# A new instruction order for a three-branch decoder layer: small products counted dearer

## The chip, the cores and the metric

The kernel runs on one core of one Trainium2 chip. The metric is device microseconds from launch to end, the median of several runs. Before the change it is 2362.93 us (three runs, 2354.34 to 2368.78).

## What is computed

One decoder layer over 2048 tokens of width 1024, float32. The normalised input goes through one projection into three groups of eight heads of width 64 each; each group mixes along the tokens in its own way, is gated, and one output projection closes the layer.

```python
h = _rmsnorm(x, norm_w[l])
proj = (h @ w_in[l]).astype(F32)
p_gdn, p_rwkv, p_hgrn = _split(proj, (GDN_PROJ, RWKV_PROJ, HGRN_PROJ))
y_a = _gdn_branch(p_gdn, ...)     # conv, l2norm, chunked delta rule, triangular solve per chunk
y_b = _rwkv7_branch(p_rwkv, ...)  # token shift, data-dependent decay, delta-rule state
y_c = _hgrn2_branch(p_hgrn, ...)  # forget gate, outer-product state
y = jnp.concatenate([y_a, y_b, y_c], axis=-1)
x = x + y @ w_out[l]
return _rmsnorm(x, final_norm_w)
```

## The kernel before, in words

**Tiling.** Tokens are cut into four blocks `tb` of 512, heads into four pairs `p`. A unit is one block and one pair, so there are 16 units, named `tb_p` (0_0 to 3_3). Chunks are 32 tokens, 16 in a block.

**Projection products.** Large products have a stationary tile of 128x128 and 512 moving columns (256 at block edges). They write the tiles `mmrr`, `mmrk`, `mmrv`, `mmgk`, `mmgq`, `mmgv`, `mmhq`, `mmhf`, `mmhi`, `mmrg`, `mmgg`, `mmhg`, `mmwa`. Weights come over DMA in pieces (`wr`), ScalarE (ACT) takes the high part (`w[:, 0]`) and GpSimd (POOL) the low part (`split`, line 496); three products (high by high, high by low, low by high) make one float32 result. Of all PE work these are the ones that wait for little: weights and a free bank.

**Small products.** Inside a unit everything is made of products on 32x32 or 64x32 tiles with 32 to 128 columns, float32, two passes each: scores `r_sc`, `g_sc`, sums `g_ss`, `r_ss`, `h_d`, the two halves of the triangular solve `pX`, `pY` (line 999), `uW`, `GA`/`GB`, `MA`/`MB`, the state chain `pc` (16 steps, line 1073), outputs `r_po`, `g_p`, `h_po`, and transposes `g_ptk`, `g_ptv`, `r_px`, `g_px`, `h_px` and others.

**The solve of a unit.** After `g_sc` on PE, VectorE (DVE) makes `GA`, scales it, runs 15 dependent steps `slv`/`Tf`, widens to `Bu` and transposes to `TT` and `Bn` (lines 1022 to 1044). `Bn` is an operand of `pX` (line 1047). Between `g_sc` and `pX` PE has no work of this chain; what the order puts there is projection products and small products of neighbours.

**Order.** The body is written as threads, and the string `ORDER` fixes how they are interleaved; both stay. Each instruction that is recorded by a `Lane` (line 243; all of them have line 253 in the profile) gets its final place on its engine from the table `LANES`: for each of five engines (PE, DVE, ACT, POOL and the DMA queue of SP) a packed permutation of the program's order. `lay_down` (line 259) unpacks it and chains neighbours:

```python
first = np.cumsum(runs[0])
order = np.concatenate([np.arange(a, a + n) for a, n in zip(first, runs[1])])
for a, b in zip(order[:-1], order[1:]):
    tc.add_manual_dep(seen[b], seen[a].name, edge, reason="lay_down")
```

The table was written by a planner outside the kernel, which priced each operation; neither its prices nor its due times stand in the file. After `lay_down` comes a last stage outside the table (lines from 1512), the second half of the output projection and the final norm.

**Head.** `derive` (line 380) makes small tiles of at most 17 columns from the parameter tile `pr` (`omu`, `hw0`, `hkk`, `hka`, `hln`, `hhn`, `hgn`, `lbx` to `olb`, `nea`) on DVE with three ACT exponentials or logarithms. `block` (line 613) loads the rows of x (`xt`), normalises and transposes them (`pxt`). `decays` (line 697) makes `tba`, `gg`, the small products `pg`, and from them on ACT `gc`, `gam`, `egc`, `egl`.

Of the kernel before, what the change touches and what calls it, by code (L numbers as in the profile page):

```python
# [48 lines left out]
def consts():  # L49
# [20 lines left out]
    for i, l in enumerate(LEVELS):  # L70
# [66 lines left out]
        "K$}Wy`8w==27I~%xaRRfdJelhD=7a8uhh`fd;^uy!+aif7DUT=8_%RSu|5eaujI|>FX2txNcU1NuA>!H$0typU!ln~nO~%UFQYZUaXLMLcPaWM"
        "FXgP$$h-I>s^`(ps{BZ2bN(PVI;->3Fu$AkQD@#ymE4Qg!}fXnYZ^@Rc@aIp*MjXFe&@i~m(%aL9sV5)c21&;!A=D=0n74ylar-w`D&*lU*|YL"
        "wwmgxm6u|#$N77}wG>#gKvqf%_=iA|1`}<(jGp9ksfBv;Cv-ZmfM2^qOXH{qJn#tpmam{cb6+q!h5Ep=)8O;hcp}tQ1FyUb3zFcqj$Ve&R)NPP"
        "EdxIzXeAWe4}AQDZsFT#CWT<Nj(gIpbPZO{p>t^@e*w>C!0-~9#fSNRtUMEJ)zTR7m4WS5w3mC(XIupY9nj|>XjAF^URYj7W4Vcz(ms9|GxNaH"  # L140
        "BXk@5G9D+NMi<h9@Y4lQ=@=;QRH(2C{3S^#yB1jY@H-f_(DTs5FtC(_2fyS>Se$3Y?on2LTEZiY%2nj})CK6ihIjU&<?(eAeVX1EK1#65aB8E6"
        "@cb0Kax3K!KPt*D<?(b0&Ea3r&4`orJQ&eC0KWV?&e*}d@x@^HaX8vg>|O$os1v7(4eb(Xo#-$;-VTdiKul~!Q#$V>bJfykr7y?IJgZ!w^!gq&"
        "zYcqT1ormB+JndmYX2V80LF)4%}VgK8)~Zt?hkk?@<<0_crSNCY(CG2xE}ZhVW)p%<w5Yd4^j9Z?4W!!11By7@~eTd18kLmtv#@NFx1g3(Y}&L"
        "<J^pJ*PCvT$g6-7@4-_Od{j>huzrCktRK#sK%RJJE_SXFb*hY#MBklqh|B@-(AgM2&EJLQx9}=%!`Y8Q(@#L%D|r;`>yE6^#k8LIb{E*zY^AZE"
        ">faQ$lpiCzQ}FKr-iJ8WESxOoPL|m*^bTw8M?fDbnuL>;r(1yGFjT)lcI$(T(PHw(KjB4Xf7Y;-7RHlBShhiRNkr9!*yl2!`4TLx1GZ<-6!!%z"
        "o#5{@a-(9k1E_rTf%rco{Y<f@9adZc9BY6<d%P=9dsyFyw{Hm-EjW8O@>3QW`z$&U^W7xAy5aOLu%ij5PeTO0#EaqKHpKE=U~C4S{y2XYs=-WB"
        "HK>#5QbkpNC~-7)u16lK1ghtFx}Z|gG7GE@p;PG<sZnW~NSmRgabmNMn$O|u8nM0%W0w?1-C;}KGL}T1iZCt&-n)>G+kov#v>N1u6?8st1h#uI"
        "p3YCv-MoSCLnc{_96d^+(L+BLUU(mVRaxsasYa0|`=S~&Bg@_+*)!lH@J)YY&9yX@*V8n9hOR;et|sO?`9|n<9&|QOD#F$9?+R3d8T2+X#2frm"
        "S`4cz>13ea2rl!y9cmtc6LXUN&qF?2&kD^1@No#<3XoyD7=Be9ehJppVm>8Iza7)4!lATN4$gMs+s}aFUGTaJI{jMSE5$4lPc}(psVZBFjL{;a"
        "nb>P4kiEdyh)TDB2krM(6K8qsnigdqWR)AXaUst7l8Ulru^20-?f9}BwsfK6v0E3!?ivo^5tVN~g~AR4Y0@%RBNqHWbv8=f*pK`&-p1SrM4GZ*"  # L150
        "AzFmo&|+}BjI8c~k*)Bg%7IxEYui}GWxe32gmo(JKZUhjB|kiEV{8gM-2(4x@2MQFGN#s9SLq!`pVKTFQT|o=VF#G1FUk*{B@Q<6Wbn2VIrN*c"
        "Gz)qEOhiSicxDoPMXU48IOPx`OGndweEkJ>&eA|A<W%gt7M1u(xx0NIm83)%R!X`Xnu|x&M6@hC-xq6!2!jg6ZW~jLu}Inj&nD?QlPOdjU5}f<"
        "If$jXd^e)0f!6`!Sk$c7_#LTO(_#5#bRA~r!uxA+kK6>+Y=yr+g11$+RKCy|{-D+1yK;h3p33Yx`_%~kt?<$|uBMA%rBB`9gU!h1dHx(x+#A0`"
        ";fp+Ut=9XpS755H&UOl2UtrbokuupZg&L&wuIkWiyy*dS+Pc5->EJku5?xb!(M?uU(`YsBQp@>IxB=GFLURLL%vVYlk4H(3t*=o{sx(>rOD?FZ"
        "8ChW{l<+8WdI#%R8H=ZVs6ril060}&jWq|j0sSr>2#xkY^q10m-%^nV<Gda4a4J?w&lc^bz-d=ttPsy%j*}<B=QHs;0D8dx2Kj$E0sPmNU*>Ge"
        "4|49x9|7*oc&ewJ`JPTGAH^;6u-whhM;xsI$G@U>ei<1r509<IJ?boE)AKM|MWcByW%*O8<_~c{^c>DN;J$MfGQ`I;j`#8goLGmO@F09s3kCfJ"
        "_sv@81AMifLuV8ZbVl&&V1GF?l>+4xyj^bUH<5~)b8t7kg>R*w^N*0T$0KT{LTST*eJB)CPd}zRxDWp0Xhk~-jFr;E@P&$<+4LLmaVh<QAHp5{"
        "X8IZB^EEV|ZpXJ-x`&^oDPV01{8NViR^F3)(uatSwb=b*iS;CIb4T$s0bZRzFS1fsD|jC$k(5SF|3qq)`rD5DwjDO!&hu#@YQP=55r{X?c;16b"
        "{y6l1CuT~(VJmhYf|aL0<sQ!V$i=KHzg5t)`VXxN?_D$>e-0goX9ukhg&3#NLiyUouZxjuMxOlo)D!P(@$Ad)KB_{9mXmd^>=DW?z8SgZH!wTu"
        "{X&c{mXRYPeTGX3^IK_J!mLV|*|dH3@S8!kD9rh2p}bWiPsW~kR{fb`L(W*Dt=D6X)H5xBP1+OMgAI6!<8v{WlQVPBlCoW|4+V8-kh|tj&&Kg7"  # L160
        "77}84M#dTJm$07J7(&4p;nclvTTb37Tp9CD<MY90&RC)Gh47*$JjW6BF??wJ5!agkoG>y&Rz$em7=OO~K5e<x=QoJ&Ju^}>;V}#pw4{6AT3_%*"
        "0=c;GRzEe!ZjR`71~8VHJ#u1$#_9=DFNV{X-zt1nCSLKxB3Jm<->CJWcum`zHVSjC1sbuoC2cKrEqaAGG~X9{$BQXBV|<b^{3qx}qp3(W%I*f)"
        "IW1pk>s-U3YqY5&MLh*_l4HL2j7M7J+h)UxLf35LFcjQ{XbX*{DXX!9LNl@G)2+%xRmNb=*c=gB-RfNv$aE2Rsn`yx=~ycRhpvr3jbEeFD%EIv"
        "q8~0O0;5u`xzKndXU@|)JvZk6==A7&HBOmvL6MPdsaPv$(6zCq`YY_2k==fb<$~4CG8<U#Yh^`%8t&RyN*ivRqP!8t?2l&<Wl5>Ey}(o==IMlG"
        "AnxyoFE2LVN%|(6k#i;*T+4-PnD8aq(iY=DlQ}AFo-7kPqEYS`93f(AhO8`$sV!}Msv{<_Sxui3pn^qTWlWxRX_U>H2~^g|LnW{;fhy|87^^h9"
        "YK&TGKCJM~UzCegzRj5WrFB#sV}+a@h#y?5$rDXA@Wpdc_VkUPG<L^iR7cJaV|Agp8bmBbJf%%8DKPAsN>Iq2`b^)dJApfC#QW9O^RC4cn7H>%"
        "4RB4~3uN}%SQaQS<l5Ti+UgcqO%Aj=O&B}0H{GH*Q_m$uG3Fjq3F6tL&@^+t$<qH@oo=k2<!sCivzbEkGtpr4VvGbuH7!EsTNSDJ>}-7+`9Bro"
        "#EbO_^X-Gix|~E+l%2yOTXmLJUuE%hoK&W7#!?}#xrVv4Ae>?2(u>`z5@NsV6Lu!5JP8wRQADMU73v<S;>S1Z3R$N%mizS6G;>y2?1m8CaP%n+"
        "!hdv6{AR`SW0lLbH!Ig_@JTb1#oP9x>=$Y80+S_@rY<SfoFI3N3ZuEuFp`Y1<6HKM73RevRe7~ixQO3O<2AJkeWTG-5L@Y*h<9zg7e|R-6o*=0"
        "rS{HOP?sw?+$~a6vBJDqev8+oIp0!|zFl+rp5fXI;DBd+n{&+?*T%e7aN1_YoW+w7u3dvEp2IwITP=(N)3h(Oy=lu+Iu=WbSSE{Vns3finbwo1"  # L170
        "P)?7m(e`-eW)K>tJaf<0G1fDNqi{<JV)`xIr3%;!xAwr;8d={>Mk>}T>`kd~!}Y;oVDe$c?&ThH_i>9NOW7XS8(^i}$&rzr{{rUP5Hk"),
# [1447 lines left out]
```

## Time and profile before

| | |
|---|---|
| median of three runs | 2362.93 us |
| profiled execution | 2368.77 us |
| its span, first to last instruction | 2367.0 us |
| PE busy | 2204.5 us (93%) |
| DVE busy | 1482.6 us (63%) |
| ACT, POOL busy | 794.9 us, 677.1 us |
| mean granted TensorE clock | 0.977 |
| DMA | 145 GB/s |

PE is busy nearly all the time; its busy time counts modelled, overlapping spans of pipelined products, so it isn't PE at its peak. The rest of the span is PE idle: 2367.0 minus 2204.5 is 162.5 us.

### The profile page before, as it was taken

The page shows a single profiled execution, that of the slowest core. Times are in us where ns is not written, and L with a number is a line of the kernel's source. Part 1 is how long each engine was busy: PE and PEld are TensorE (multiplying, and loading weights), DVE is VectorE, ACT ScalarE, POOL GpSimd, SP SyncE. Part 2 cuts the span into 40 slices and gives each one's busy share as a digit, 9 for nine tenths or more (in the row PEclk, how much of TensorE's full clock was granted, in tenths as well). Part 3 has the DMA queues.
Part 4 walks back from the last instruction along what each step waited for, and adds up shares of the span by engine and source line. Part 5 has one row for each costly group of instructions (what it writes and reads, how often), then busy time and mean ns, then how long its engine had stood idle before and what let it go on. Part 6 is the DMA issues. An engine that isn't in the chain of part 4 may idle for free.

```text
span 2367.0 us, 86943 instructions
## 1 busy us (share of the span) xinstructions
PE 2204.5 (93%) x38264; PEld 1757.6 (74%) x38264; DVE 1482.6 (63%) x3430; ACT 794.9 (34%) x1586; POOL 677.1 (29%) x993
## 2 busy tenths in 40 slices
...
PEclk8999999989999999999999999999999999999999
...
GB/s 150 170 178 156 179 158 182 177 150 103 139 123 114 121 109 124 127 165 110 156 87 144 91 140 102 166 132 136 122 127 118 113 131 127 180 154 217 237 231 156
DMA packets 236363, 343.16 MB, mean 145 GB/s; under 512 B 22608, under 2 KB 99792, under 8 KB 235984
## 3 DMA queue, kind: packets, MB, share of 16 engines
...
q8 instruction: 300, 4.92, 0.9%
...
## 4 chain that ended last, share of the span: by engine, by line
PE 72%; DVE 14%; issue 5%; DMA 4%; ACT 3%; POOL 2%; SPq 0%; ACTq 0%; POOLq 0%; DVEq 0%
PE pa L253 6%; PE pc L253 5%; PE mmrk L253 4%; PE mmhq L253 4%; PE mmgv L253 4%; PE mmgq L253 4%; PE mmrv L253 4%; PE mmgk L253 4%; PE mmhf L253 3%; PE mmrr L253 3%; PE uW L253 3%; DMA wry<-ydram 2%; PE mmhi L253 2%; PE r_po L253 2%; DVE Tf L253 2%
## 5 line engine op out<-in xcount | busy, mean ns | idle before, releaser
L253 PEld LDWEIGHTS pc<-S,M 128*128 128x128 f32 x1024 | 145.1, 191 | 28.6 <-DVE S L253 6.7
L253 PE MATMUL pc<-S,M 128*128 128x64 f32 x1024 | 149.8, 269 | 3.0 <-DVE M L253 1.7
L253 DVE TENSOR_TENSOR S<-pc,S 128x128 f32<-128x128 f32 x256 | 73.4, 287 | 82.8 <-PE pc L253 79.8
L253 POOL TENSOR_TENSOR wy<-wry,wy 128x256 fp32r<-128x256 f32 x96 | 71.8, 759 | 92.1 <-ACT wy L253 90.6
L253 POOL TENSOR_TENSOR D<-gw,cst 128x512 f32<-128x512 f32 x64 | 71.4, 1116 | 83.7 <-DVE rawhg L253 34.1
L253 DVE SCALAR_TENSOR_TENSOR h_S<-h_S,tot 128x64 f32<-128x64 f32 x256 | 83.1, 325 | 14.9 <-ACT h_S L253 10.4
L253 PE MATMUL pa<-hhi,wy 128*128 128x512 f32 x224 | 74.3, 412 | 3.1 <-ACT wy L253 2.5
L253 ACT ACTIVATE wy<-wry 128x256 fp32r<-128x256 f32 x96 | 38.7, 416 | 113.7 <-DMA wry<-ydram 77.0
L253 DVE TENSOR_TENSOR Tf<-Tf,slv 128x15 f32<-128x15 f32 (+7 forms) x240 | 63.8, 266 | 6.4
L253 ACT ACTIVATE uW<-uW 128x1024 f32<-128x1024 f32 x32 | 32.8, 1025 | 95.3 <-PE uW L253 95.3
L253 DVE TENSOR_TENSOR slv<-Af,Tf 128x15 f32<-128x15 f32 (+7 forms) x240 | 60.5, 252 | 6.1
L253 PEld LDWEIGHTS h_l<-h_q,h_k 64*32 64x32 f32 x4096 | 41.4, 106 | 25.4 <-issue 12.2
L253 POOL TENSOR_TENSOR g_n<-g_n,mhalf 128x8 f32<-128x8 f32 x16 | 26.6, 1660 | 110.4 <-DVE g_n L253 110.4
L253 POOL TENSOR_TENSOR h_e<-h_k,h_q 128x512 f32<-128x512 f32 (+1 forms) x32 | 36.8, 1149 | 70.8 <-DVE h_q L253 46.6
L253 DVE COPY_PREDICATED h_P<-mlev,h_l 128x128 f32<-128x128 int32 x128 | 37.3, 296 | 27.0 <-PE h_l L253 26.8
L253 PE MATMUL h_l<-h_q,h_k 64*32 64x32 f32 x4096 | 48.8, 200 | 4.6 <-issue 2.4
L253 DVE TENSOR_TENSOR h_k<-h_k,tot 128x256 f32<-128x256 f32 x64 | 32.6, 510 | 32.3 <-PE h_l L253 32.0
L253 PE MATMUL pa<-whi,yl 128*128 128x512 f32 x128 | 50.0, 391 | 3.0 <-DVE yl L253 3.0
L253 DVE TENSOR_TENSOR M<-MA,D 64x512 f32<-64x512 f32 x64 | 43.9, 686 | 11.5 <-PE MB L253 8.9
L253 PEld LDWEIGHTS pa<-hhi,wy 128*128 128x128 f32 x224 | 41.6, 195 | 12.6 <-ACT wy L253 3.0
L253 PE MATMUL pa<-whi,yh 128*128 128x512 f32 x128 | 49.9, 390 | 0.1
L253 PE MATMUL pa<-wlo,yh 128*128 128x512 f32 x128 | 49.8, 389 | 0.0
...
## 6 DMA issues: line engine op xcount, KB each, us to landing
...
```

Of the source, the lines that this page charges most:

```text
L253: i = f(*a, **k)
```

## The change

Only the five packed strings in `LANES` are replaced. No instruction is added or removed: each table holds the same number of entries (22140 on PE, 3338 on DVE, 1515 on ACT, 973 on POOL, 1292 on SP). The packed text says nothing to a reader, so here is its shape, and then what comes out when it is unpacked and put beside the names of the recorded instructions.

```diff
 LANES = {
     "tensor": (
-        "c-nne36vGZ6@C4?fB)aJ;Gba|0j1#&GXuji0R;vSz77t{3@D>9ic3&*Jg(r8C?d%@F^VBZ;xQ(e=rJ+JEU38Q7MFyhqEQqO1R;Q86xkFN!Xg>|"
...
+        "c-nPV4RBP|6+XLf_w8<WldK7Z<xid@Bq0!pAb%~$5+H#D1T0cUElmr>3JA2;pQ43UEwoA*oZ25OgO=&Eb&9ARtU{R%+B#YRg|W&gMlG!fEiEde"
...
     "vector": (
...
     "scalar": (
...
     "gpsimd": (
...
     "sync": (
```

Instructions with another neighbour ahead of them than before: 1555 on PE, 1931 on DVE, 683 on ACT, 329 on POOL, 169 on SP. On PE a middle instruction is displaced by 6 places or fewer in half of the table, and by 296 at most.

**Projection products between the last `g_sc` and the first `pX` of a unit** (those of 256 columns count one half), units 0_0 to 3_3:

| | 0_0 | 0_1 | 0_2 | 0_3 | 1_0 | 1_1 | 1_2 | 1_3 | 2_0 | 2_1 | 2_2 | 2_3 | 3_0 | 3_1 | 3_2 | 3_3 | sum |
|---|---|---|---|---|---|---|---|---|---|---|---|---|---|---|---|---|---|
| old | 114 | 108 | 108 | 45 | 120 | 123 | 90 | 75 | 120 | 120 | 111 | 67.5 | 108 | 111 | 120 | 40.5 | 1581 |
| new | 111 | 111 | 96 | 39 | 117 | 114 | 81 | 73.5 | 108 | 126 | 87 | 60 | 108 | 120 | 108 | 51 | 1510.5 |

Counted from the product `pe` to `pX` the sums are 1482 and 1438.5, from `g_ptv` to `pX` 931.5 and 913.5, from `pX` to `pY` 123 and 118.5, from `pY` to the first `uW` 97.5 and 114. The small products inside the first of these stretches are nearly the same in both tables. DVE instructions from the last `GA` of a unit to its `Bn`, all units: 970 and 966.

**Stretches of small products** with no projection product and no transpose in them: 104 of 128 passes or more in the old table, 116 in the new; 13 and 20 of 192 passes or more.

**Head.** On SP the first part of `pr` moves behind the first tile of x, and the second part behind `wba`. On DVE the old order has `hw0`, `hkk`, then the first product row (`xt0_20`), then `xm0_3`, `omu`, `hka`, `lbx`, `hln`, `hgn`, `nea`, `hhn`, the difference `hlo`, the rows `xt0_30`, `xt0_31`, then `lbr`, a row, `lbs`, `lb`, `olb`; the new one has `hw0`, `xm0_3`, `omu`, the row `xt0_20`, `hkk`, `xt0_30`, `hka`, `xt0_31`, `hlo`, and only then `hln`, `hhn`, `nea`, `hgn`, `lbx`, `hka`, `lbr`, a row, `lbs`, `lb`, `olb`. On ACT the order `nea`, `hhi`, `lbe`, `hhi`, `olb`, weight split `w3wa` is the same; later the old order has `gc`, two `gam`, `egc` ahead of the split `w2wa`, and the new one has the splits `w2wa`, `w3wa`, `w0rr` ahead of `gc`. On PE the three `pg` stand ahead of the products with `w2wa` in the old order; in the new one two `pg`, three products with `w2wa`, the third `pg`, then the rest.

## Rows read from the trace of the kernel before

**Rows 1.** The page, part 1: the span, then busy time by engine.
```profile
span 2367.0 us, 86943 instructions
PE 2204.5 (93%) x38264; PEld 1757.6 (74%) x38264; DVE 1482.6 (63%) x3430; ACT 794.9 (34%) x1586; POOL 677.1 (29%) x993
```

**Rows 2.** The page, part 2: granted clock in 40 slices, in tenths.
```profile
PEclk8999999989999999999999999999999999999999
```

**Rows 3.** The chain that ended last, shares of the span by engine.
```profile
PE 72%; DVE 14%; issue 5%; DMA 4%; ACT 3%; POOL 2%; SPq 0%; ACTq 0%; POOLq 0%; DVEq 0%
```

**Rows 4.** Windows: busy time of each engine in head and tail, first the columns.
```profile
core 0: us, PE busy (x) PEld busy (x) DVE busy (x) ACT busy (x) POOL busy (x), PEclk, DMA share, GB/s
0.00:50.00 50.00, 27.67 (x246) 23.44 (x246) 22.60 (x58) 26.68 (x69) 16.06 (x42) 0.90 0.48 156
...
2050.00:2200.00 150.00, 141.57 (x1262) 110.23 (x1244) 52.56 (x99) 40.30 (x100) 74.58 (x94) 0.97 0.63 190
2200.00:2367.00 167.00, 151.32 (x648) 123.02 (x648) 80.97 (x93) 49.57 (x68) 18.63 (x28) 0.97 0.62 205
```

**Rows 5.** Waits of PE: total us, times, longest; by what was waited for.
```profile
PE pX L253 <- DVE Bn L253: 17.5, 13, 3.0
PE pxt L253 <- DVE xt L253: 16.5, 6, 7.4
PE g_p L253 <- issue: 10.4, 7, 2.0
PE GB L253 <- issue: 5.8, 3, 2.6
...
PE r_po L253 <- issue: 4.1, 3, 2.1
...
PE pY L253 <- issue: 4.0, 3, 1.7
```

**Rows 6.** Timeline of PE in the head: start, duration, what, idle before.
```profile
23.93 0.39 PE L253 MATMUL mmwa_0h<-hhi,w3wa_0h 128*128 128x256 f32 x1 [4.00 <-ACT w3wa_0h L253]
...
41.28 0.60 PE L253 MATMUL pg<-gg,cst 128*128 128x32 f32 x4 [4.10 <-issue]
...
44.48 0.58 PE L253 MATMUL mmwa_0h<-hhi,w2wa_0h 128*128 128x256 f32 x1 [2.30 <-ACT w2wa_0h L253]
```

**Rows 7.** Timeline of ACT in the head.
```profile
23.36 0.20 ACT L253 ACTIVATE olb<-olb 128x4 f32<-128x4 f32 x1
...
42.23 0.22 ACT L253 ACTIVATE gc<-pg 128x64 f32<-128x64 f32 x1 [1.49 <-PE pg L253]
...
44.03 0.41 ACT L253 ACTIVATE w2wa_0h<-wr2wa_0h 128x256 fp32r<-128x256 f32 x1
```

**Rows 8.** Timeline of SP in the head: the DMA issue of the parameters.
```profile
1.19 0.42 SPq L253 DMA_DIRECT2D pr<-par  x1
```

**Rows 9.** Timeline of PE around the first solve product of unit 1_2.
```profile
905.63 0.39 PE L253 MATMUL mmhg<-hhi,w1hg 128*128 128x512 f32 x1
...
906.99 0.39 PE L253 MATMUL mmhg<-hhi,w2hg 128*128 128x512 f32 x1
909.99 1.29 PE L253 MATMUL pX<-Bn,ATo 32*32 32x32 f32 x128 [2.61 <-DVE Bn L253]
```

**Rows 10.** The tile Bn: who writes it on DVE, 16 times.
```profile
L253 DVE STREAM_TRANSPOSE Bn<-Bu x16: 1040/1070/1135, 138.9 to 2016.3; 128x512 f32<-128x512 f32 x16
```

**Rows 11.** Timeline of PE: two groups of 16 small passes.
```profile
213.15 0.40 PE L253 MATMUL r_po<-uW,r_TL 32*32 32x64 f32 x16
...
213.60 0.40 PE L253 MATMUL r_po<-uW,r_TL 32*32 32x64 f32 x16
```

**Rows 12.** The page, part 3: the queue that brings instructions.
```profile
q8 instruction: 300, 4.92, 0.9%
```

**Rows 13.** Windows around two of the waits of Rows 5, columns as in Rows 4.
```profile
1026.00:1037.00 11.00, 7.28 (x273) 6.36 (x273) 8.12 (x15) 4.26 (x10) 2.35 (x5) 0.69 0.45 150
1530.00:1540.00 10.00, 7.50 (x285) 6.82 (x286) 7.22 (x13) 3.60 (x8) 2.48 (x5) 0.83 0.40 133
```

More of the change, by code (lines that the diff above doesn't have):

```diff
@@ L137 @@
[L137 to L171, printed above, removed]
@@ new lines @@
+        "S;cu03zY5O<E%~Zg1d<qJiA5r9lsJqWZcF-skN*-$9q2cF|@ajtX7M>o`B(Ob9CGb>QPF)w<lYTsKdWc_-Ca5p9=Ku1*e3gKmW9CRAec=#hB+x"
+        "^{gtmtC`cz;HfXVn|X>Z6}mH+-TI?n8F8da{U6{y1q1"),
+    "vector": (
+        "c-o~{S&ST46}|J`tKMfHk3D0I?TIa9659|5oR~Ev3P@r5Kp;L4;)6s22@psm`GhYNP*5Zg2!8lLLV(}{gjm9sMcKeM2}{CiX8}9TjK|LGz0Bp@"
+        "`(9O7*Hrg(+Zw&@>Z-Tgd+t5w-kKp|wp5@NN7TfXAsH<;_#B~SuF^VJ@I8!Ss758Kv&_BBV;GYp^B7OwOuxt6TKLuE0_~<vp1`UG)^746bR73A"
+        "{+gJ#mlk*j&0|=4Nw4<Nb9{jQ&99|r_z3-(XX!kbu+CyQ*f&Z`_$|9fu+D{Ziqv3#RiO=?YjJN4&l$6um}_zW0R0y;*5JnsPT5C`u<JRVqZfG("
+        "MgvzDxQ^?ySZB%6H0BrdT!w86Jf$lZ!gUEdF7XJ?ndfPet2I0^dbPx(@OU#=Ql(Y+zKY+&ilF~x=~m2k^mELAC;fy!KtEFa9%jMT(J*{!@Z<C;"
+        "{sZ4YC;5H!GdzDU{glO`IpDPm_8!FPf@ckDYQSeD;84bIIlZLzx44LJu|u9ntXA-pS>jy=K8B{?liVMJkMemLt7`b%g>z(|2(u^E|4TfMF+mZ2"
+        "P2zMHqBDWjmzXuyBYMIxa>j<($gCowx1gUZ9oR^2dF!gc&;nWU-~>I+@-6u|iam}1gX8ohpQJnZ6yFS-3>~Jw@L~EZON8G}5Av<_8@`jig?RYA"
+        "Dm1B{3POb>i@ZNg&7fj(*Wuh%V7P)IUM?#_RYaLt(A<Hjiai$lR^eZRWrbw8L)I-}H(A@jj;u%);Z+%{%NpekM54u`ipo5$$AN2+1j#zS$HLx{"
+        "A7agJJeB;K(o9=I=AKOu`yl<0KTJQs@6XYFd=EVQJa+gJ-J@1Iuyr0+a&`%}E@Cf<+99AhhR;iUo@bCZyXl;IG)=DnC5hH3ypM2I$2_kEavcTV"
+        "EcsZp*yC8o{@$Loz!syc7`7CEjSPz&M=(?3S?A9nE>?L9SCvyv_pIs+&&xHet_POLn1$ch(0@`x@Hm^~+}^<5J@h}|Ay=Xi64^R3caeobRiOMb"
+        "{FD=Fcvd9gainLDVqRL2B031|IY|G~@f!Mve#^<Pqo<UGHvvb<v}ui~tdQ*W>p8Kj9Q3FXz9Vv~r5u!%Rk^%=iA9lm-$EWs%tUFY>3QCdENH;T"
+        "bE<;z?mJ<<>@cPXy@Kz$=8Dtk_{@_m9ML?B6{m)oZN|w}MbBJU#8??Bdp7tNbPK<p{>0Z~FuwtNJ{_1QjNHn!b@jHOOsiqff-*_GFsi<uDN-wn"
+        "2^uz+YcXpq?VyW_l;@kQn9#^y!tTRZ)l4$72-ZoKEo<hC!OLUNgCq2Jcx^TA^IBId#j%O6EZt7O<ac4b2bg@HKT6-_SQjRd^B=<RN9kAm1+{rZ"
+        "6~#wuMs;-qzvCSx+r96RUVG0s1J0YkaZ@=trdBT_rq5%?ae6`huHlI&4fBR_xSaTHaMnxU>w>a>68<<6&8=XTJS_wjb95Z}DXWjFB0h^Vj?*8J"
+        "txsZ{3Rvs}?}g9adq<z7Z{TV#o_vJ9i6?iWHr&s5(Y<^x-NpAoS0(~0JonC^LZ0DU=y&`MRQa1R_8?A^+5>FB3$e&EzkpMGJiV%|BVs%7Dd<Yp"
+        "IjkF1q%J4*->ZUT<A!=B%oYAhF0E?31@%wB<`!4Ax=CJa1{EnN+cq>Va!M&&OO8oC?uJ6_Ms`U3nS+9O%OnmmtX9W$mRu6V8H~FC%xA#6S&jTA"
+        "e3A%9fh%I$!*nATl+ThC*I?KE7=n>>Fh}WW?Pg>MpF}y{LXQBirrK?3ME&x5D)y8SNuM)C?CFt|4BuqWmug4lc3NASs@YBKDoSt>zK((=h9uTI"
+        "HUE8|U?{%YsdyWm>ovFlZ{n)9uD1A`iYxXM=0-HCO0p7ID^`@lm7%z1%jt{kV|N{W1xj)Z*>{XitCF0~RBWl{Z=;8hQNQIo=-aSrO*6ZQ9GA1Q"
+        "S|V69*>kO5C6SKtVu+eeeU4+rNKnu?PfemIYub%?%@j=${kk4j9|g1WxO6*KRq1>DG5QXFoDR_4-0m?%OCF>X$_cCX&jw{Eke}g4g+#&Xs@7gd"
+        ";%tain|<wwEp@6a;>!xZT6?k=IPR(&+|pc<is0+5Lq0617D^Vlge!uzkHk}<Gd_a&Y@pITiw^uGzfmjRsg#zw93A~MeI3>Pe!d&A_+rwtiLNyG"
+        "%TST8(r2-5B3QQvUG=MAg;bLhu;dBEU7{!UL_tG@x%;*5onx;g)7r&&%smE+ut)5WUPe0D^Y|`nrbtZ1w~A(v^u%SYk7cOG*McTz^&_q|z7Mt9"
+        "-3z;#s@qaUBixI763NfG!0mWAjns_d>-(Y#e2%S_?pQLamC=zFve5VWHz||j_ad)L`}F<f3>YK*;UpMzf*#|yqW7KJq9W<Hp*CaMZ*=j~l5*XK"
+        "^R4E9M?sW)TorvWbR6<2tGsUXt0K~mG(xv%R84%}-_9K0pVmWF^j)&=6MY}zw3jYWwih|glAmv)NA(@(TKXFwLZ)_VNWc9^P5D*OY?J3psv;xc"
+        "`-@vN#3Sb`a}<!82yb|@s--<}zIv=8hmLh<M_x}NzSyKPd)|t2oT9^OO}hV>)1KgE?c*f|7ebvnr(J4#2v@2!t4xx;J)@)+-T*9*k+7*q(trLq"
+        "@tM`?%lbCyv7ANpntGbol7?oQ?_8Dwe`L@1qn8prSw(Gc>Ra#{zZ;%k2Yesk+vwN4tUjy(2dQK6dxythSb5geK5kO8@S;|=N_d-hxG(QQ@+t9^"
+        "o<ury>B?`UC$zTShI0f7(L=H5GGB|&L-bFr$Wz$EzX$sh8ystiyytoqmflL#*Y}t8@V^F$avZ6cV^Xi@=oz*l|82;Ca?nOUtFCHL2uzSn8p6CG"
+        "{WD>-e`WvDGc0V1?-%v6nwm9(6Fb*BeIhe!IlE@>h;5xSq8xjMdRp7<?qIu^j1ODyM}6&W`<i2VT2u{p#?=<n^>owKb29)YdAZ;Q#?*V|20D2w"
+        "+Wo|{7G{Wk#<}YH_N+HT@m-r*mEL`DRPxriT&DH2lj%UalEY=2pd-WNAYoFTrFR|Nx2R*C$-z77xvRZOHm6n1riSZ4*=79Q{%<s_vKfT(tTa9I"
+        "DjVMzeVgmOSHs>6YRAtF#LX+w)sb+DOPChh-j9m*6VWshHYX!ZN-Mq3HsoEmD%PD*wlD488DfyVZ-T8R6MNGGQPWlDyX954+)3xJO}J+>=h%)o"
+        "b=SqMe8}^t8lqp`VpsVJRIpbB%r?kHeKEHf>Q;VUx*qXz9lBvNy^QU%s>jNat{rY02J~N-21D3&^cbec?6w}6ZPnIYVcg@Y?KGCf6h^jdl^$G4"
+        "(hRXZ)HClC8+5KamwIP%d*!a&o~E<j+HG^7pN`IDv@?6k&=$SQ*3CldxyfK-dR9%B!`Ncd!KZtSN=mD?T3Q~c9`&bXSI44Kq6Ybz)a!kzv;XKk"
+        "(Iyye|2LMw$@Y=?z3bm#edeGlVtT$Wn2x#jDl}xckAB2#t01OlFWId#>#iOyr5)S7bF}Ao)4Xb`9u4*2aJnv=ocP(EeMi358XCHSF0tQ;mU38C"
+        "8ZbArZ!hhdG?D5Hx6kg*C{;2u3OUunBt1r2ztgrm+Cl#Z1Mq~h"),
```

129 lines of the change are left out of this document (62 added, 67 removed).

## The prediction

> **What bounds the kernel now.** I read the page first: PE is busy 2204.5 of 2367.0 us, DVE 1482.6, and no other engine is near [rows 1]. The chain that ended last says the same: 72% of it is PE's own work, 14% DVE's [rows 3]. The work itself isn't changed by a new order, so what the order can win or lose is PE's idle time, 2367.0 - 2204.5 = 162.5 us, and what the granted clock takes. The clock row shows full speed in most slices [rows 2]; its mean of 0.977 is worth 0.023 x 2367 = 54 us of the span if PE was busy all that time.
>
> Next I split the idle time. The windows give the head (first 50 us) 50 - 27.7 = 22.3 us, and the tail from 2050 us on (150 - 141.6) + (167 - 151.3) = 24.1 us [rows 4]. The waits of PE give two heaps in the middle: the solve products `pX` waited 17.5 us for DVE's `Bn` in 13 of the 16 units, and where the releaser is "issue" (PE waited for nothing that the profile shows) the four longest heaps `g_p`, `GB`, `r_po`, `pY` make 10.4 + 5.8 + 4.1 + 4.0 = 24.3 us [rows 5]. The rest, 162.5 - 22.3 - 24.1 - 17.5 - 24.3 = 74.3 us, is spread over many small waits. The reader should see that there is no large hole: 1% of the run is 23.6 us, more than either heap.
>
> **The solve windows.** This is the place where the old order's fit can be read. In 1_2 PE is through with its projection products at about 907.2 us and then stands 2.61 us until `Bn` is there [rows 9]. That `pX` waits in 13 of 16 units, but only 1.3 us on the mean and never over 3.0, shows that the old order has the two sides nearly level, PE a little early and DVE a little late. The new table takes projection products out of these windows: 70.5 fewer counted from `g_sc`, 43.5 fewer counted from `pe`, 18 fewer counted from `g_ptv`, while DVE's stretch from `GA` to `Bn` stays at 966 instructions against 970. That is what a dearer price for the small products would do: the same chain on DVE seems covered with fewer large ones. One projection product takes 0.227 us (six steps from 905.63 to 906.99 us [rows 9]), so PE arrives earlier by 70.5 x 0.227 = 16.0, 43.5 x 0.227 = 9.9 or 18 x 0.227 = 4.1 us in sum. `Bn` itself, a transpose of 1.07 us, comes no sooner [rows 10]. I take the middle anchor, +10 us of waiting, since DVE's chain runs from `pe` on by way of `E` and `GA`; the ends +4 and +16 stay for the range.
>
> [...]
>
> **Where the products go.** They stand elsewhere, since none is lost. From `pY` to `uW` there are 16.5 more (3.7 us), and no wait of `uW` is among the long ones [rows 5]. The others may stand ahead of one of the spread waits. Bounds: nothing, or all of the 9.9 us taken out of the solve windows. No row is nearer to either end; I take half, -5 us.
>
> **The issue waits.** The instruction queue brought 300 packets, 4.92 MB [rows 12], and PE's 38264 products and as many weight loads [rows 1] are 255 instructions for each packet. The waits called issue stand inside runs of small products [rows 5], which at 14 ns a pass use up the 128 passes of one packet in 1.8 us [rows 11]. Runs of at least 128 such passes go from 104 to 116, a factor of 1.12: 24.3 x 0.12 = +3 us. Runs of at least 192 go from 13 to 20: 24.3 x 0.54 = +13 us. I take +3, because the small groups are the same ones in nearly the same neighbourhood.
>
> [...]
>
> **The head.** The first part of `pr` takes 0.42 us on SP ahead of x [rows 8]; without it x starts at most 0.4 us sooner. The wait of 4.00 us for the split `w3wa` hangs behind `olb` on ACT, 23.36 us [rows 6, 7]. The new order puts `lbx`, the root of `olb`, later among the rows, and `xm0_3` and the rows earlier; these are operations of 0.1 to 0.7 us on either side, so I leave this wait as it is. The third wait goes: PE stood 2.30 us for the split `w2wa`, which ACT did at 44.03, behind `gc`, which had waited 1.49 us for PE [rows 6, 7]; now the split stands ahead of `gc`. The wait of 4.10 us ahead of `pg` stays, since `pg` needs `gg` and nothing ahead of `gg` is moved by much. At best -2.3 - 0.4 = -2.7 us, at worst 0, if the weights behind are late next; I take -2. If ACT's three splits delay `gc`, its dependants `gam` and `egl` are needed only in the next stage, so nothing on PE waits at once.
>
> **The tail.** Output products and the loads behind them keep their order but for the places near the last unit; I cost it at nothing, bounds -3 and +3, by the wait of `pa` that would move with it, which is under the 24.1 us of rows 4.
>
> **The sum.** -2 + 10 - 5 + 3 = +6 us. On the profiled execution's own 2368.8 us that is 2374.8; this execution lies 5.8 us above the median of the runs, so for the median 2362.9 + 6 = 2369 us.
>
> **The rivals.** A, faster: the table, made with truer prices, fits everywhere else, and half of the 74.3 us of spread waits goes, while solve, issue and head are as above: -37 + 10 + 3 - 2 = -26, 2337 us. For it speaks that these waits are many and short, so small shifts can close them; against it, that in the one place where I can measure the fit the shift goes the wrong way. It decides from 35 us of such waits closed (35 - 11 = 24), so nearly all of it is needed.
>
> B, slower: the solve waits grow by the whole 16 us of the `g_sc` anchor, nothing comes back elsewhere, and the longer waits pull the clock down. Around 1026 us the granted clock is 0.69 for 11 us, 3.4 us lost, and around 1530 us 0.83 for 10 us, 1.7 us lost, each time at a wait of PE [rows 13]. Eight units whose wait grows over 2 us would cost 8 x 1.7 = 14 us. 16 + 14 + 3 - 2 = +31, 2394 us. It passes 1% from the fourth such unit on (17 + 4 x 1.7 = 24). Against it: PE does more work in other windows and may meet DVE later everywhere.
>
> C: the issue waits take +13, not +3: +16, 2379 us. D: small products that alternate with other work take more than the 14 ns they take in a row [rows 11], so the new cover, with the same small products in it, is as long as the old one seemed: -2 + 0 - 5 + 3 = -4, 2359 us. [...] E: the changed parts of the head do nothing, since the weights set it: +8, 2371 us, which can't be told from the forecast.
>
> **How the numbers follow.** Forecast with E 0.42, C 0.08, D 0.10: together 0.60 for within 1%, which is about what a measurement here can tell from no change (2339 to 2387). A holds 0.20, B 0.20. The forecast's own range is 2355 to 2382. The range for 8 in 10 reaches from A to B, 2337 to 2394, and leaves out the further half of each.
>
> **What would show it.** Right: PE's busy time within 5 us of 2204; `pX` waits for `Bn` in all or nearly all units, 22 to 33 us in sum; no wait for `w2wa` over 1 us in the head; issue waits of 25 to 38 us. Wrong: a sum for `pX` under 17 us refutes the counting of the cover, and with it the sign; a granted clock under 0.965 means B; an idle time of PE under 140 us means A.

## The result and the profile after

The new order takes 2385.38 us (median of four runs, 2380.03 to 2388.15); the kernel before, beside it on the same chip, takes 2358.64. The ratio is 1.0105 [1.0074, 1.0136]. In a second comparison (run `again`, below) it was 1.009 [1.0064, 1.0116] with 2386.94 against 2365.74 us. So the change costs about 1%, 21 to 27 us. The time lies in the predicted range, in its upper part; the likeliest value, 2369, was missed by 16 us, and the time is also above the forecast's own range (2355 to 2382).

The page after, in the lines that answer to [rows 1 to 3]: span, busy time, granted clock in 40 slices, and the chain by engine.

```profile
span 2385.9 us, 86941 instructions
...
PE 2223.1 (93%) x38264; PEld 1772.9 (74%) x38264; DVE 1474.9 (62%) x3430; ACT 797.3 (33%) x1586; POOL 677.5 (28%) x993
...
PEclk9999999989999999999999998899999999899999
...
PE 68%; DVE 17%; issue 5%; DMA 4%; ACT 3%; POOL 3%; SPq 0%; POOLq 0%; ACTq 0%; DVEq 0%
```

PE's idle time is 2385.9 - 2223.1 = 162.8 us against 162.5 before: no change. PE's busy time rose by 18.6 us for the same 38264 passes, and that is the whole of the longer span (18.9 us). The same work took longer because the granted clock was lower:

```profile
core 0: 2385.9 us, clock 0.969
```

Against 0.977 before, that is (0.031 x 2385.9) - (0.023 x 2367.0) = 74 - 54 = 20 us. This pair of profiles gives the clock the most: over eight timed runs of the new order (1 - clock) x span is 66 us on the mean, over 25 runs of the old 57 us, so the clock's share over all runs is nearer to 10 of the 21 to 27 us. The other 11 to 17 us lie outside the clock, and this pair of profiles hides them: the profiled execution of the kernel before (2368.77 us) was the slowest of its four, 10 us above their median. The second profile of the new order (run `again`) is 15.9 us longer than the old order's: 8.7 us by the clock, 3.1 by waits over 0.1 us, and some 4 us that stay without a place.

The waits of PE, as in [rows 5]: total us, times, longest.

```profile
PE g_p L244 <- issue: 18.5, 10, 3.1
...
PE pX L244 <- DVE Bn L244: 12.4, 9, 3.0
PE GB L244 <- issue: 7.6, 6, 2.6
PE r_po L244 <- issue: 5.8, 5, 1.9
...
PE pX L244 <- DVE xm L244: 3.1, 1, 3.1
```

`pX` waits less than before, not more (12.4 + 3.1 = 15.5 against 17.5 us). The waits called issue grew: `g_p`, `GB` and `r_po` had 20.3 us, now 31.9; the fourth heap of [rows 5], `pY`, fell from 4.0 to 1.6. Summed from the trace between 115 and 2125 us ("the middle" from here on: PE's idle times over 0.1 us), issue waits went from 34.4 to 44.4 us and all other waits from 72.2 to 66.6.

**Where the time was lost.** I matched each product with itself in the other trace and compared its start. Up to 1440 us the new order lags by -2 to 8 us, back and forth; from there the lag grows steadily to 22 us at 2050 us. Windows of that stretch, kernel before and after (columns as in [rows 4]; each first the kernel before, then the new order):

```profile
1400.00:2125.00 725.00, 691.50 (x13516) 558.25 (x13514) 468.75 (x1153) 228.67 (x443) 180.04 (x258) 0.99 0.46 135
```

```profile
1400.00:2125.00 725.00, 686.89 (x13357) 554.16 (x13356) 458.36 (x1138) 223.08 (x429) 169.04 (x244) 0.96 0.43 129
```

The reader should see the clock column: 0.99 against 0.96 in 725 us is 22 us. The old order has 13.7 us at half clock (a granted clock of 0.50; the clock records of both traces hold only 1.00 and 0.50) in this stretch, the new one 58.0.

One place shows both sides. In unit 2_2 the new order has the 192 passes of `GA` and `GB` in one run; the old one has three passes of `mmrk` and the product `pz` after the first 64. Timeline of PE, first the new order, then the old (start us, duration, what, idle before):

```profile
1430.42 0.22 PE L244 MATMUL GB<-uW,r_TL 32*64 32x64 f32 x1
1433.22 0.27 PE L244 MATMUL GB<-uW,r_TL 32*64 32x64 f32 x1 [2.59 <-issue]
...
1433.94 0.69 PE L244 MATMUL mmrk<-hhi,w0rk 128*128 128x512 f32 x1
...
1435.41 2.07 PE L244 MATMUL pz<-lor,wlr 64*128 64x512 f32 x2
```

```profile
1429.47 0.50 PE L253 MATMUL mmrk<-hhi,w0rk 128*128 128x512 f32 x1
...
1430.36 1.12 PE L253 MATMUL pz<-lor,wlr 64*128 64x512 f32 x2
...
1433.01 0.27 PE L253 MATMUL GA<-uW,r_TL 32*64 32x64 f32 x2 [0.54 <-issue]
...
1433.77 0.50 PE L253 MATMUL mmrk<-hhi,w1rk 128*128 128x512 f32 x1
```

Both orders stand at the same count of passes, 24454 and 24453 from the first product, and go on 1.40 and 1.33 us after a 16 KB packet of the instruction queue (`q8`) has landed: there a packet of instructions ends. The new one stands 2.59 us, the old one 0.54. From 128 passes earlier to the end of the stand both take 4.2 us; the old order works for 3.7 us of them, the new one for 1.6. Behind the longer stand PE runs at half clock: `pz` takes 2.07 us instead of 1.12. Windows of the same 14 us, after and before:

```profile
1433.00:1447.00 14.00, 13.78 (x197) 7.75 (x198) 4.48 (x11) 4.47 (x8) 0.33 (x2) 0.54 0.12 40
```

```profile
1433.00:1447.00 14.00, 13.99 (x351) 10.31 (x351) 8.35 (x18) 5.85 (x10) 2.03 (x4) 1.00 0.34 97
```

That is 197 passes against 351 in the same time, at a granted clock of 0.54 (0.50 from 1435 us on) against 1.00.

**My theory then.** By [rows 1, 12] a packet of the instruction queue carries 255 instructions on the mean, 127.5 passes with their weight loads; I write 128. A stand is an idle time of PE with the releaser issue. All 66 issue waits over 0.1 us in the middle of the two traces (29 and 37) end 1.1 to 1.6 us after a packet of that queue has landed; before the other waits of PE there the last landing is 5.7 to 5.9 us back in the median. At the 20 stands over 1 us behind the head, the time from 128 passes earlier to the end of the stand is 3.2 to 5.2 us in all but three (6.9 to 8.2 us, which one time per packet doesn't explain); the median is 3.9. So, as my estimate from these stands, PE has to be busy for about 3.9 us per packet; the 128 small passes in a row ahead of 12 of the stands last 1.4 to 1.9 us, and PE stands for the rest. Where a packet's end falls inside a long run of small products it costs about 2 us (1.5 to 2.6 at these 12), and behind 10 of the 20 stands the granted clock falls within 4 us. The rivals: the order is a little worse everywhere; the stands belong to certain products, not to packet ends; the clock fell by chance; the head is at fault.

### The profile page after: what moved, and what is told of

Same layout as the page of the kernel before. It is cut to its first block, busy times and chain, and to the rows that moved or that the text cites. A ratio compares the mean times of both kernels' runs of the same rounds, so it can differ in the third digit from the quotient of the medians.

```text
span 2385.9 us, 86941 instructions
## 1 busy us (share of the span) xinstructions
PE 2223.1 (93%) x38264; PEld 1772.9 (74%) x38264; DVE 1474.9 (62%) x3430; ACT 797.3 (33%) x1586; POOL 677.5 (28%) x993
## 4 chain that ended last, share of the span: by engine, by line
PE 68%; DVE 17%; issue 5%; DMA 4%; ACT 3%; POOL 3%; SPq 0%; POOLq 0%; ACTq 0%; DVEq 0%
PE pa L244 6%; PE pc L244 4%; PE mmrk L244 4%; PE mmhq L244 4%; PE mmgv L244 3%; PE mmgq L244 3%; PE mmgk L244 3%; PE mmhf L244 3%; PE mmrr L244 3%; DMA wry<-ydram 3%; PE uW L244 3%; PE mmhg L244 2%; PE mmrv L244 2%; PE g_p L244 2%; PE pb L244 2%
## 5 line engine op out<-in xcount | busy, mean ns | idle before, releaser
L244 PEld LDWEIGHTS pc<-S,M 128*128 128x128 f32 x1024 | 146.1, 192 | 34.5 <-DVE S L244 9.9
L244 DVE SCALAR_TENSOR_TENSOR h_S<-h_S,tot 128x64 f32<-128x64 f32 x256 | 86.9, 340 | 11.4 <-ACT h_S L244 7.1
L244 DVE COPY_PREDICATED h_P<-mlev,h_l 128x128 f32<-128x128 int32 x128 | 37.7, 296 | 49.5 <-PE h_l L244 49.4
L244 PEld LDWEIGHTS pa<-hhi,wy 128*128 128x128 f32 x224 | 41.5, 195 | 13.7 <-ACT wy L244 3.5
L244 PE MATMUL pa<-wlo,yh 128*128 128x512 f32 x128 | 49.8, 389 | 0.0
```

Source lines behind the costliest of these rows:

```text
L244: i = f(*a, **k)
```

## The experiments

In the table, "issue" and "other" are PE's waits in the middle of the one profiled execution of each kernel, and "clock" is (1 - granted clock) x span, the mean over the timed runs. The kernels before that ran beside them have 57 to 58 us there.

| kernel | ratio to the kernel before | median us | issue | other | clock |
|---|---|---|---|---|---|
| before | | 2358.6 to 2366.1 | 34.4 | 72.2 | 57 |
| new order, first comparison | 1.0105 [1.0074, 1.0136] | 2385.4 | 44.4 | 66.6 | 69 |
| again | 1.0090 [1.0064, 1.0116] | 2386.9 | 44.9 | 67.0 | 64 |
| old1400new | 1.0070 [1.0046, 1.0094] | 2383.4 | 40.8 | 72.1 | 66 |
| new1400old | 1.0009 [0.9992, 1.0027] | 2369.3 | 35.9 | 68.5 | 55 |
| newhead | 1.0004 [0.9979, 1.0028] | 2364.5 | 34.5 | 72.4 | 58 |
| old_pad32 | 1.0058 [1.0032, 1.0085] | 2379.2 | 42.8 | 67.2 | 58 |
| old_pad112 | 0.9990 [0.9971, 1.0009] | 2361.8 | 29.0 | 73.5 | 57 |
| new_pad32 | 1.0027 [1.0008, 1.0046] | 2370.8 | 45.6 | 64.0 | 55 |
| new_pad112 | 1.0008 [0.9990, 1.0026] | 2366.0 | 37.7 | 71.5 | 53 |
| new_pad128 | 1.0084 [1.0057, 1.0112] | 2385.5 | 40.4 | 70.1 | 61 |
| new_one | 1.0064 [1.0047, 1.0081] | 2380.9 | 46.5 | 65.7 | 59 |
| new_all | 1.0040 [1.0023, 1.0056] | 2375.1 | 14.8 | 95.1 | 49 |
| old_all | 0.9956 [0.9939, 0.9973] | 2357.2 | 17.2 | 82.2 | 55 |

### Where in the run: the same order again, and three splices

A splice takes, on every engine, all instructions that had begun by a certain time in one order, and the rest in the other order. At 1400 us both orders have done the same instructions on each engine, but for one or two.

```diff
 LANES (old1400new; on PE 13934 of 22140 entries, on DVE 2163 of 3338)
   first part: old order up to 1400 us of the old trace
-  rest: old order
+  rest: new order
 LANES (new1400old): the other way round
 LANES (newhead): new order up to 60 us (PE 216, DVE 62, SP 49 entries), then the old order
```

again: 

> The new table unchanged, once more, with a second profile. Theory A (the loss belongs to the order: long runs of small products make PE stand with the releaser issue, and the granted clock falls behind these stands): again 20 to 30 us over the kernel before, and the issue waits and the half-clock stretches stand at the same products as in the first profile, the lag of the new order again made between 1400 and 2100 us. Theory B (the clock falls by chance of the execution, not by the order): the time again about +20 us on the mean, but the half-clock stretches at other places, and the lag spread over other stages.

old1400new: 

> All five engines take the old order up to 1400 us of the old trace, and the new order behind it. Theory A (local loss: the new order's products lag by at most 7 us up to 1440 us and by 22 us at 2050 us): 2380 to 2386 us, nearly the whole of the loss. Theory B (spread loss, each stage is a little worse): about 40% of it, 2366 to 2371 us.

new1400old: 

> The new order on all engines up to 1400 us of the new trace, and the old order behind it. Theory A (local loss behind 1400 us): 2357 to 2364 us, within 1% and hardly above the kernel before. Theory B (spread loss): about 60% of it, 2372 to 2377 us.

newhead: 

> Only the head is new: the order of all engines up to 60 us (the small derived parameters behind the first rows, and pr behind the first rows of x on SP), the old order behind it. Prediction's step for the head: -2 us, 2355 to 2359 us, no w2wa wait over 1 us. Rival (the head does nothing, since other waits are late next): 2358 to 2361 us. Rival (the head carries part of the loss): over 2364 us.

The loss isn't chance: in its second profile the new order stands 2.59 us in `GB` of unit 2_2 once more, 16 of its 20 stands over 1 us come back at the same count of passes, and the same 14 us have a granted clock of 0.51:

```profile
1433.00:1447.00 14.00, 14.00 (x165) 7.84 (x158) 4.48 (x11) 4.47 (x8) 0.33 (x2) 0.51 0.16 40
```

It isn't spread either. The part behind 1400 us brings 0.70% of the 0.9 to 1.05%, the part ahead of it 0.09%, which can't be told from nothing. In microseconds new1400old (2369.3) lies above the range of its theory A, 2357 to 2364, and newhead (2364.5) where the head would carry part of the loss; but these ranges were set around 2358.6 us for the kernel before, which took 2365.7 beside these runs, so the ratios are what counts. By them new1400old agrees with theory A (-0.1 to +0.2%) and not with B (0.6 to 0.8%); old1400new, 0.70% [0.46, 0.94], lies between A (0.9 to 1.2%) and B (0.3 to 0.5%). The windows of the two splices, old1400new and then new1400old:

```profile
1400.00:2125.00 725.00, 684.94 (x13431) 551.98 (x13430) 463.27 (x1150) 224.13 (x431) 170.72 (x246) 0.97 0.45 129
```

```profile
1400.00:2125.00 725.00, 693.26 (x13518) 559.72 (x13516) 467.65 (x1145) 229.39 (x446) 181.30 (x259) 0.99 0.46 136
```

The head alone does nothing that can be measured (-0.2 to +0.3%). Its wait for `w2wa` is gone, as predicted, but the one ahead of `pg` is longer than in [rows 6]; timeline of PE in newhead:

```profile
24.36 0.58 PE L252 MATMUL mmwa_0h<-hhi,w3wa_0h 128*128 128x256 f32 x1 [3.31 <-ACT w3wa_0h L252]
...
43.40 1.03 PE L252 MATMUL pg<-gg,cst 128*128 128x32 f32 x4 [4.82 <-issue]
...
49.01 0.38 PE L252 MATMUL mmrr_0h<-hhi,w1rr_0h 128*128 128x256 f32 x1 [0.64 <-ACT w1rr_0h L252]
```

### Is it the packet's end: passes put ahead of everything

A few passes of constants are put ahead of PE's first product, while it waits for x. All later products then stand elsewhere against the packets, and nothing else changes: 32 passes add 63 instructions to the profile, a quarter of the 255 of a packet.

```diff
+                    if tb == 0 and b == 0 and c == 0:
+                        for _ in range(16):   # 16: 32 passes; 56: 112; 64: 128
+                            nc.tensor.matmul(pq[0:32, 0:32], cst[0:32, 0:32], cst[0:32, 0:32], start=True, stop=True)
                     for k in range(4):
                         tr(pt[:, k], xt[:, 128 * k:128 * k + 128], ident)
```

old_pad32: 

> The old order, with 32 passes of a 32x32 product of constants ahead of PE's first product, where PE waits for x anyway; their result is overwritten. All later products then stand 32 passes later against the 128-pass packets in which PE's instructions arrive. Theory A (PE stands where the 128 passes of one packet last less than the 3.2 to 4.7 us that a packet takes, so the stands depend on where packet ends fall in the order): counted over the old trace the issue waits rise from 34 to about 52 us, and with the clock behind them the time to 2385 to 2400 us. Theory B (the stands belong to certain products of the order, wherever they stand): issue waits 32 to 37 us, time within 5 us of the kernel before.

new_pad32: 

> The new order with the same 32 passes ahead. Theory A: counted over the new trace the issue waits rise from 44 to about 56 us, time 2400 to 2412 us. Theory B: issue waits 42 to 47 us, time within 5 us of the new order without them, 2382 to 2391 us.

old_pad112: 

> The old order with 112 such passes ahead, which is the same as packet ends 16 passes later. Theory A: issue waits fall from 34 to about 27 us, time 2345 to 2357 us, a little faster than the kernel before. Theory B: issue waits 32 to 37 us, time within 5 us of the kernel before.

new_pad112: 

> The new order with 112 such passes ahead. Theory A: issue waits fall from 44 to about 35 us, as many as the old order has without passes, time 2368 to 2378 us. Theory B: issue waits 42 to 47 us, time 2382 to 2391 us.

new_pad128: 

> The new order with 128 passes of constants ahead, one whole packet, so that every later product stands to the packet ends as without them. Theory A (what the 32 and the 112 passes changed is where packet ends fall): stands at the same products as in the new order, 128 passes later, 2.6 us in GB of unit 2_2 again, time 2380 to 2391 us. Theory B (passes ahead help in themselves, by an earlier start of PE or a warmer clock, whatever their number): 2364 to 2374 us, as with 32 and 112.

Without any change in the order of the work, 32 passes make the old order 0.58% slower and the new one 0.6 to 0.8% faster than it was; with 112 passes both are level with the kernel before (-0.10% and +0.08%). With 128, a whole packet, the new order has its loss back (+0.84%). So it isn't the passes as such; it is where the packets end. With the same 32 passes ahead the new order is even the faster of the two. The stands say the same. With 128 passes ahead they are at the same products, 128 or 129 passes later: `GB` of unit 2_2 at pass 24582 instead of 24454, `g_p` at 25860 instead of 25731, `r_po` at 27899 instead of 27771. With 32 passes they stay near the same counts (7247, 12093, 16426, 25732, 32742) where another small product now stands. At 24454 there is none: that count now lies 111 passes into the run of `GA` and `GB`, not 143, so that six large products stand in the packet and its 128 passes last 3.2 us instead of 1.6. And it holds for all kernels: if the packet ends are read off the 20 stands of the first profile (127.5 passes apart on the mean), all 473 issue waits of the middle in the fourteen profiles lie within 7 passes of such an end. Timeline of PE in new_pad128 at `GB` of unit 2_2:

```profile
1427.29 0.21 PE L244 MATMUL GB<-uW,r_TL 32*64 32x64 f32 x1 [2.05 <-issue]
```

The sizes were mostly off. Only new_pad128 met its time, with 2.05 us, not 2.6, at its stand in `GB` of unit 2_2. old_pad32 and the two with 112 passes went the way of theory A with other sizes: issue waits of 42.8, 29.0 and 37.7 us where I had counted 52, 27 and 35, and times 6 us below, 5 us above and 2 us below the ranges; old_pad112 by its time alone can't be told from no change. new_pad32 went the other way: my count gave 56 us of issue waits and 2400 us or more, measured were 45.6 us and 2370.8. The count took one packet time for all packets, and it left the clock to follow the issue waits, which it didn't: with as many issue waits as the new order, this kernel lost 55 us to the clock, not 66. In old_pad32 it was the other way round, +8 us of issue waits at an unchanged clock; since its other waits fell by 5 us, most of the 16 us that it lost stay without a place. So how much clock a stand costs depends on the place.

### One stand, and all of them

In new_one PE's table is changed at one place: four passes of `mmrk` and one `pz` (two passes; the expectation says eight and a `pz`) go into the 192 passes of `GA` and `GB` of unit 2_2. In new_all the same is done at 17 stands, in old_all at 11 of the old order.

```diff
 PE order, unit 2_2 (new_one)
   GA, GB  64 passes behind the packet's start
+  mmrk x3, pz x1, mmrk x1
   GA, GB  rest, over the packet's end
-  mmrk x3, pz x1, mmrk x1
   mmrk x2, h_l ...
 new_all, old_all: about 12 passes of projection products from behind
   each run of small products go 64 passes ahead of the packet's end in it
```

new_one: 

> The new order, changed at one place of PE's table alone: eight passes of projection products and a pz product that stood behind the 192 passes of GA and GB of unit 2_2 go between these passes, 64 passes ahead of the one at which PE stood 2.6 us in all three profiles of this order. Theory A (the packet is late because 128 small passes are through too soon, and 13.7 us of half clock hang on this stand): the stand falls under 1 us, the half-clock stretch of 13.7 us behind it goes or shrinks to one of 3.4, time 5 to 9 us under the new order, 2377 to 2381 us. Theory B (the clock there falls for another reason): the stand goes but the half-clock stretch stays, time 2383 to 2388 us.

new_all: 

> The new order, changed in the same way at 17 of the 18 places where PE stood over 1.2 us with the releaser issue (32.7 us in sum): about 12 passes of projection products that stood behind the run go 64 passes ahead of the packet's end. Theory A: two thirds or more of the 32.7 us go, and half clock with them: issue waits in the middle 15 to 25 us, time 2345 to 2365 us. Theory B (PE would stand somewhere else instead, for DVE or ACT, because the small products come later): issue waits fall, waits for DVE and ACT rise by as much, time 2380 to 2390 us.

old_all: 

> The old order with the same mend at its own 11 places (20.3 us of stands; nothing moved at four others). Theory A: issue waits in the middle fall from 34 to 15 to 22 us, time 2335 to 2352 us, faster than both kernels. Theory B: within 5 us of the kernel before.

The one stand shrinks from 2.59 to 0.40 us, and the half clock behind it is gone. Timeline and window of new_one:

```profile
1431.69 1.12 PE L240 MATMUL pz<-lor,wlr 64*128 64x512 f32 x2
...
1434.43 0.27 PE L240 MATMUL GA<-uW,r_TL 32*64 32x64 f32 x2 [0.40 <-issue]
```

```profile
1433.00:1447.00 14.00, 12.82 (x400) 9.16 (x400) 7.53 (x19) 6.53 (x11) 1.85 (x4) 1.00 0.26 79
```

400 passes now run in the 14 us, against 197. The ratio falls from 1.0090 or 1.0105 to 1.0064, 6 to 10 us for five instructions; the intervals overlap, so the times alone don't show the gain. The sum of issue waits didn't fall, since other stands were longer in this profile; what came back is clock (59 us lost against 66).

new_one leaves a rival: it also breaks up the run of small products, and the run itself, not the stand, could pull the clock down. The other kernels decide it, since in several the same 192 passes follow each other unbroken. Where PE stands among them (2.58 us in old1400new, 2.10 in new_pad112, 2.05 in new_pad128), 13.7, 10.2 and 13.7 us at half clock follow. In new_pad32 it doesn't stand in them, and the clock stays up; window of new_pad32 from the run's end on:

```profile
1418.60:1432.60 14.00, 14.00 (x320) 9.42 (x313) 8.30 (x20) 6.64 (x11) 2.57 (x4) 1.00 0.36 97
```

So at this place it is the stand at the packet's end that pulls the clock down, and 13.7 us at half clock cost nearly 7 us, more than the 2.6 us of the stand. new_pad112, though, is level with the kernel before with this stand in it; its gain came from other places.

new_all is the lesson on the other side. Issue waits fall by 30 us, but other waits rise by 28, most of them for `Q`, a tile that DVE makes (24.0 us in the middle, against 2.6 in the new order). Its time lies between the ranges of the two theories, and its profile is of its slowest execution (2384.05 us). Waits of PE in new_all:

```profile
PE r_px L242 <- DVE Q L242: 14.9, 9, 2.7
PE pX L242 <- DVE Bn L242: 12.9, 8, 3.2
PE g_p L242 <- DVE Q L242: 6.3, 6, 2.0
```

The projection products that I moved into the `g_p` runs had covered the time in which DVE makes `Q` for `r_px`; that wait isn't among the long waits of the new order. PE stands as long as before, only for DVE. The gain of 0.5 to 0.65% (11 us) is no more than what the clock gives back, 49 us lost against 66.

old_all, the same on the old order, is 0.44% faster than the kernel before (0.9956 [0.9939, 0.9973]), some 9 us, and so faster than both orders. I had expected 11 to 28; here too part of the stands turned into waits for `Q` (11.4 us in the middle, against 1.7).

## Why the prediction was right in the range and wrong in its steps

The range held, but the way there was luck: the largest term of the sum had the wrong sign, and the two terms that carry the loss stood in it as +3 us and as nothing. Of the signs that the prediction named for being right, PE's busy time failed (2223.1 us, not within 5 of 2204) and the sum for `pX` too; the wait for `w2wa` and the four issue heaps (33.5 us, in 25 to 38) were met. One reading was wrong without consequence: 1% of the run, 23.6 us, is more than the heap of `pX`, but not more than the 24.3 us of the issue heaps.

**Head, -2 us: about -1.** The wait for `w2wa` went, and no other one over 1 us for it came; `w3wa` fell to 3.3, `pg` rose from 4.10 to 4.82 us. Summed, PE's head waits fell by 0.9 us, and newhead shows no gain.

**Solve windows, +10 us: -2.** This is the step that failed, and the text had named the mark: a sum for `pX` under 17 us. It was 15.5, and this isn't chance: the old order has 17.2 to 17.6 us in four profiles (as it is, with the new head, with 32 and with 112 passes ahead), the new order 14.6 to 16.0 in five. PE did come earlier, by 1.64 us a unit on the mean (from the last `g_sc` to the first `pX`, 31.32 to 29.68 us without the wait), more than the 10 us in sum that I took. But `Bn` came earlier too, by 1.71 us (32.27 to 30.56). I had taken DVE's stretch as unchanged because it has 966 instructions against 970. Counted in time it isn't: DVE's busy time between `GA` and `Bn` fell by 0.78 us a unit, with 3.0, 2.3 and 2.8 us in units 0_3, 1_2 and 2_2, because longer instructions went elsewhere, and DVE stood 0.2 us a unit less in between; the other 0.7 us were gained ahead of `GA`. The planner had moved both sides together; I had counted one.

**Moved products, -5 us: -3.6** (other waits in the middle without `pX`, 54.7 to 51.1). Near in sign and size, but not shown to be an effect of the moved products: passes ahead of the old order alone move the same sum to 49.8 and 56.3 us.

**Issue waits, +3 us, bound +13: +10.** The mechanism was right, the term was taken near the wrong end of its bounds. The 14 ns a pass in it come from two groups of 16 passes of `r_po` that began at 213.15 and 213.38 us, with the next one at 213.60 ([rows 11] shows the first and the third): 0.45 us for 32. I took the factor of the runs of 128 passes or more (1.12) and not that of 192 or more (1.54), because the groups seemed to have the same neighbours. The `GA`/`GB` run of unit 2_2 shows what that missed: the same group, once split by `pz` and once not. Rival C had the size, +13, with a chance of 0.08. But with 32 and with 112 passes ahead the new order has only 2.8 and 8.7 us more issue waits than the old one, so part of the +10 is where the packets happened to end.

**Tail, nothing: -4 us**, 14.3 to 10.3 us of waits; the other kernels, old order and new, have 8.7 to 16.4 there, so this is no effect of the order.

**Clock, nothing in the sum: +10 to +20 us.** It stood only in rival B, as a consequence of longer `pX` waits (1.7 us a unit). The clock did fall, to 0.969 in the profile, near the 0.965 that I had set as the mark for B, but mostly not behind `pX`. If each fall of the clock in the middle is put down to the wait of PE just ahead of it, the time at half clock behind issue stands went from 30.7 us to 51.2 and 54.6 in the two profiles of the new order, which costs 10 to 12 us; behind `pX` it went from 10.2 to 13.7 in both. Behind other waits, for weights and tiles of other engines, it went from 34.1 to 61.4 us in the first profile, but to 34.1 in the second: this part of the +20 is one execution's and not the order's. Rival B had the right second half on the wrong first half; C had the right first half and left the second out. Put together, the two profiles of the first comparison give +10 for the stands, -10 for all other waits (head -1, `pX` -2, the rest of the middle -4, tail -4) and +20 for the clock: the 19 us between the spans.

**Issue waits as a property of the order.** My sum took it that a longer run costs more, wherever it lies. The shifted kernels show that most of the 1% hangs on where the packets end. With 0, 32 and 112 passes ahead the old order has 0, +0.58 and -0.10%, the new one +0.9 to +1.05, +0.27 and +0.08%. The means are +0.16 and about +0.44%; with three places each, the difference of 0.3% isn't settled. So the change by itself, apart from its luck with the packets, may be close to the +6 us that I forecast, or to nothing.

**Rivals A, D, E.** A (faster) needed 35 us of spread waits; they fell by 4. D (small products dearer when mixed, so that the cover is as long as before) isn't borne out: the cover got shorter by 1.64 us a unit, and PE's work at full clock is the same within 1 us in the first pair of profiles (span less waits over 0.1 us less half the time at half clock: 2158.7 and 2157.9 us; 2162.8 in the second profile of the new order). E, a head that does nothing, was right, and couldn't be told from the forecast.

**Left open.** Why the clock falls behind some stands of 2 us and not behind others, and for how long, was not settled: behind a stand of 2.62 us in `GB` at 1550 us of the old order, and one of 3.30 us at the same product in newhead, it fell for 3.4 us only. Where the 11 to 17 us outside the clock lie in the runs that weren't profiled is open too. Nor was settled the gain of a mend that takes its products from further off, so that `Q` stays covered.
